# Layer B's attention: a step's filling work ahead of its scores, queries one step later, the output's first pieces two by two

## The chip, the cores and the metric

The kernel runs on one core of one Trainium2 chip. The metric is the device time of one execution in microseconds (us), and for the kernel before it is the median of three runs.

## The reference

A trunk of two layers, 512 tokens, 1024 features, float32. Layer A is latent attention with an MLP behind it, layer B is windowed attention with an MLP behind it; every sublayer is followed by a scaled residual and a layer norm. The change lies in layer B's attention, so that is what is shown (cut):

```python
def _swa(x, w_q, sinks, w_o, k_band, v_band, rel_bias):       # 16 query heads, 4 key/value heads, 64 wide
    q = (x @ w_q).reshape(B, nb, BLOCK, SWA_KV_HEADS, G, SWA_HEAD_DIM)
    s = jnp.einsum('bnqkgd,bnjkd->bnkgqj', q, k_band) * SWA_HEAD_DIM ** -0.5   # block of 128 queries, 256 keys
    s = jnp.where(mask, s + bias, -jnp.inf)
    m = jnp.maximum(s.max(-1), sink)
    p = jnp.exp(s - m[..., None])
    p = p / (p.sum(-1) + jnp.exp(sink - m))[..., None]
    o = jnp.einsum('bnkgqj,bnjkd->bnqkgd', p, v_band).reshape(B, S, 1024)
    return o @ w_o
```

`k_band` and `v_band` hold, for each block of 128 tokens, the keys and values of that block and of the one before it.

## The kernel before

Every product is made of rounded halves: an operand is split into a high half (ScalarE, a copy) and a low half (VectorE or GpSimd, a subtraction), both by the helper `split` (lines 77 and 81), and three matmuls stand for one product, by the helper `group` (line 105). In the profile line 105 is therefore nearly all of TensorE, and lines 77 and 81 are the two halves of a split, told apart by the tile that they write.

TensorE runs its instructions in the order of the program. On the other engines the order is fixed when the kernel is built, by a list of priorities in which earlier code goes first, except where `behind(...)` orders one instruction after another.

Layer B's attention goes head by head in `run_steps`. A unit is a head, `AHEAD_B` is 2, and the steps are u = -2 to 15. In a step stand, for the 16 heads:

- `scores(u + 2)`, here S(u+2): eight matmuls into two PSUM tiles of the tag `mm` (six tiles of that tag for everything). Behind them, off TensorE: four adds of the bias with a maximum (VectorE, line 1332), one small operation `nb` (line 1336), four exponentials (ScalarE, line 1340), a fifth one `ri` (line 1344), a sum and a reciprocal (VectorE, lines 1345 and 1346) and two scalings of `p` (GpSimd, lines 1347 and 1349). The last exponential of line 1340 is kept as `state["exp"]`.
- the filling work, a list of closures with a weight and a due step each. `queries(m, part)`, here Qm.0 and Qm.1: twelve matmuls each, and with the second part the load of a bias tile and the split of the queries of heads 2m and 2m+1 (ScalarE line 1303, VectorE line 1304). `more_values(t)`, here V2 and V3: 24 narrower matmuls each and a split. `proj.part(t, kp)`, here Pt.kp: six matmuls of the output projection, into one PSUM tile for each block t that stays held until the projection ends. P0.2, P1.2 and P2.2 read the attention output of heads 8 to 11.
- `turn(u)`, here T(u): seven transpositions of `p` (lines 1360 and 1362) into two PSUM tiles of the tag `tr`, of which there are two in all, and a split of each into `pth` (ScalarE) and `ptl` (VectorE). The first tile takes four transpositions, the second three.
- `mix(u - 1)`, here M(u-1): eight matmuls with the values, then `low` (ScalarE, line 1391) and `o` (VectorE, line 1392), and after each second head a split into `oh` (ScalarE) and `ol` (GpSimd).

The split of T(u)'s first tile is ordered behind the newest exponentials in the program:

```python
if k2 == 0:
    with behind((state["exp"],)):
        split(pth[:, 0:2, :], ptl[:, 0:2, :], pt)
```

At that point of the program the newest exponentials are those of S(u+2). `fill` is worked off by weight: a closure is called while the weight spent is below the share due by the step, or its own due step has come.

Weights come as a stream: when a chunk is taken, the chunk three further on is loaded (SyncE) into one of two raw tiles and split into one of four pairs of tiles `wh`, `wl`. The chunks of the query weights and the first three of the output projection have their low half made on GpSimd, the later ones on VectorE.

Of the kernel before, what the change touches and what calls it, by code (L numbers as in the profile page):

```python
# [25 lines left out]
SQH, SKVH, SHD = 16, 4, 64  # L26
# [15 lines left out]
AHEAD_S, AHEAD_B = 3, 2  # L42
# [6 lines left out]
def build(tc, nc, io, out):  # L49
    with ExitStack() as top:  # L50
# [11 lines left out]
        def nm(s):  # L62
            n_names[0] += 1
            return f"{s}_{n_names[0]}"

        def bank(cols=512, tag="mm", bufs=6):
            return ps.tile([P, cols], F32, tag=tag, bufs=bufs, name=nm(tag), padded_shape=[P, 512])
# [35 lines left out]
        def group(dst, pairs, first=True, last=True, **kw):  # L103
            for i, (st, mv) in enumerate(pairs):
                pe(nc.tensor.matmul(  # L105
                    dst, st, mv, start=first and i == 0, stop=last and i == len(pairs) - 1, **kw
                ))

        def three(sh, sl, mh, ml):
            return [(sh, mh), (sh, ml), (sl, mh)]  # L110
# [197 lines left out]
        def weights(name):  # L308
            i = state["at"]
            state["at"] += 1  # L310
            while state["next"] < len(stream):
                on_ring = len([j for j in range(i, state["next"] + 1) if not off_ring[j]])
                if on_ring > AHEAD or state["next"] >= state["hold"] or (off_ring[state["next"]] and mlp_pool[0] is None):
                    break
                prep(state["next"])
                state["next"] += 1
            got, wh, wl = ready.pop(i)
            assert got == name
            return wh, wl
# [7 lines left out]
        class Feat:  # L327
# [11 lines left out]
            def turn(self, t):  # L339
                turn_tokens(t, self)  # L340
# [189 lines left out]
                    for t in range(NT):  # L530
                        self.evac(t, slice(512, D), bs[t])

        def run_steps(units, ahead, scores, turn, mix, fill, per, lag, rest):

            total = sum(f[0] for f in fill)
            n, spent, at = len(units), 0.0, 0
            for u in range(-ahead, n):
                if u + ahead < n:  # L540
                    scores(*units[u + ahead])
                target = total * (u + ahead + 1) / (n + ahead)
                while at < len(fill) and (spent < target or fill[at][1] <= u) and fill[at][2] <= u:
                    fill[at][3]()
                    spent += fill[at][0]
                    at += 1
                if u < 0:
                    continue
                turn(*units[u])
                if u >= lag and (u - lag) % per == per - 1:  # L550
                    mix(units[u - lag][0])
            for f in fill[at:]:
                f[3]()
            for f in rest:
                f()
            for u in range(n, n + lag):
                if (u - lag) % per == per - 1:
                    mix(units[u - lag][0])
# [29 lines left out]
        def feat_major(src, w, dst, cols=slice(0, S), ks=range(KD)):  # L588
            wh, wl = w
            for k in ks:  # L590
                kc = slice(k * P, (k + 1) * P)
                group(dst, three(wh[:, kc], wl[:, kc], src.h(k, cols), src.l(k, cols)), k == 0, k == KD - 1)
# [30 lines left out]
        class Factors:  # L623
# [6 lines left out]
            def scratch(self):  # L630
                return self.mp.tile([P, 4, 256], F32, tag="uv", bufs=3, name=nm("uv"))

            def sum(self, n, a11, a12, a21, a22):
                if n == 5:
                    self.a = self.scratch()
                    nc.vector.tensor_sub(self.a, a21, a22)
                    return self.a
                if n == 3:
                    nc.vector.tensor_sub(self.a, self.a, a11)
                    self.b = self.scratch()  # L640
                    nc.vector.tensor_add(self.b, a12, self.a)
                    return self.b
                if n == 7:
                    nc.vector.tensor_sub(self.b, a11, a21)
                    return self.b
                return {1: a11, 2: a12, 4: a22, 6: self.a if n == 6 else None}[n]
# [250 lines left out]
        with tc.tile_pool(name="mla", bufs=1) as mp:  # L897
# [222 lines left out]
            def scores(h, i):  # L1120
                a = heads[h]
                kk = a["k"]
                qh, ql = a["q"]
                n = (i + 1) * P
                tq = slice(i * P, n)
                b = bank()
                p = scratch()
                mask = cmask[:, 512 - n :]
                if i == 0:

                    two = b[:, 0:256].rearrange("p (a b) -> p a b", a=2)
                    group(
                        two, [(qh[:, tq], kk[:, :, :n]), (a["qr"][:, tq], krr[:, :, :n])], True, False,
                        skip_group_check=True,
                    )
                    group(b[:, :n], [(ql[:, tq], kk[:, 0, :n])], False, True, skip_group_check=True)
                    nc.vector.tensor_add(p[:, :n], b[:, n : 2 * n], mask)
                    mask = p[:, :n]
                else:
                    group(  # L1140
                        b[:, :n],
                        three(qh[:, tq], ql[:, tq], kk[:, 0, :n], kk[:, 1, :n])
                        + [(a["qr"][:, tq], khh[:, :n]), (a["qr"][:, tq], kll[:, :n])],
                    )
                if i == 0:
                    for name in ("mx", "nb", "sm", "ri"):
                        a[name] = sp.tile([P, NT], F32, tag=name, bufs=3, name=nm(name))
                mx, nb, sm, ri = a["mx"], a["nb"], a["sm"], a["ri"]
                one = slice(i, i + 1)
                nc.vector.tensor_tensor_reduce(  # L1150
                    out=b[:, :n], in0=b[:, :n], in1=mask, op0=ALU.add, op1=ALU.max,
                    scale=1.0, scalar=NEG, accum_out=mx[:, one],
                )
                nc.vector.tensor_scalar(nb[:, one], mx[:, one], -MLA_SCALE, None, ALU.mult)
                nc.scalar.activation(
                    p[:, :n], b[:, :n], AF.Exp, bias=nb[:, one], scale=MLA_SCALE, accum_out=sm[:, one]
                )
                nc.vector.reciprocal(ri[:, one], sm[:, one])
                nc.vector.tensor_scalar(p[:, :n], p[:, :n], ri[:, one], None, ALU.mult)
                a["p", i] = p  # L1160
# [17 lines left out]
            def mix(h):  # L1178
                vh, vl = v_h[h // 4], v_l[h // 4]
                vc = slice((h % 4) * P, (h % 4 + 1) * P)  # L1180
                pth, ptl = heads[h]["pt"]
                b = bank()
                for kb in range(NT):
                    c = slice(kb * P, S)
                    group(
                        b[:, c], three(vh[:, kb, vc], vl[:, kb, vc], pth[:, kb, c], ptl[:, kb, c]),
                        kb == 0, kb == NT - 1,
                    )
                split(oh[h // 4][:, h % 4, :], ol[h // 4][:, h % 4, :], b)
# [9 lines left out]
            fill = []  # L1199
# [32 lines left out]
        with tc.tile_pool(name="swa", bufs=1) as mp:  # L1232
# [55 lines left out]
            def queries(m, part):  # L1288
                if part == 0:
                    qb[m] = (weights("w_sq"), bank())  # L1290
                w, b = qb[m]
                feat_major(x2, w, b, ks=range(4 * part, 4 * part + 4))
                if part == 1:
                    load_bias(m)
                    with tc.high_priority():
                        query_parts(m, slice(0, S), b)
# [100 lines left out]
            fill = []  # L1397
            for m in range(2, 8):
                for part in range(2):
                    fill.append((2.6, 2 * m - AHEAD_B - 3 + part, -9, lambda m=m, part=part: queries(m, part)))  # L1400
                if m == 2:
                    for t in range(2, NT):
                        fill.append((2.6, 0, -9, lambda t=t: more_values(t)))
            for t, kp, u in ((0, 0, 11), (0, 1, 12), (1, 0, 13), (1, 1, 13), (2, 0, 14), (2, 1, 14), (0, 2, 15), (1, 2, 15), (2, 2, 16)):
                fill.append((1.3 if t < 2 else 0, u, u, lambda t=t, kp=kp: proj.part(t, kp)))
            begin(
                x2, ["w_k"] * 2, [lambda cols, b, m=m: keys(m, cols, b) for m in range(2)],
# [2 lines left out]
            for m in range(2):  # L1410
                for part in range(2):
                    queries(m, part)
            run_steps([(h, 0) for h in range(SQH)], AHEAD_B, scores, turn, mix, fill, 1, 1, [])

        gb = lambda: load_gb("mix", 1)
        with tc.tile_pool(name="mlp1", bufs=1) as mp:
# [114 lines left out]
```

## Time and profile before

| | |
|---|---|
| runs | 997.11, 997.43, 998.21 us; median 997.43 us |
| the profiled execution | 997.58 us, of which 995.8 us are the span of its instructions |
| granted TensorE clock | 0.999 |
| TensorE busy | 983.9 us (99% of the span) |
| VectorE, ScalarE, GpSimd busy | 772.3, 555.2, 215.4 us |

Times of rows are microseconds from the start of the span. A row of a timeline has start, duration, engine, line, operation, the tile written and the tiles read, shapes, a count, and in brackets the idle time before it with what ended it. A row of the chain has start, duration, engine, tile and line. A row of stretches has the stretch, its length, the busy time of TensorE, of its weight loads, of VectorE, ScalarE and GpSimd with instruction counts, the granted clock, the share of the DMA engines and GB/s. A row of waits has who waited for whom, the total, the number of times and the longest. A row of groups has line, engine, operation, tiles, shapes and count, then the total busy time and the mean in ns.

### The profile page before, as it was taken

Reading aid. Unit: us, or ns where it says so; the run is one execution under the profiler, and the core shown is the slowest. Engines: PE = TensorE matmul, PEld = TensorE weight load, DVE = VectorE, ACT = ScalarE, POOL = GpSimd, SP = SyncE. Lnnn points to the kernel's source line nnn. Section 1 sums busy time; section 2 is a strip of 40 time slices with the busy share of each in tenths; the row PEclk is TensorE's granted clock in tenths of the full one; section 3 lists DMA queues with packets and bytes.
Section 4 is the critical chain, followed back from the end, with each engine's and each line's share of the span. In section 5 each row is a group of like instructions: output and inputs, shape, how many; then the busy total and the mean of one; then the engine's idle time right before and its main releaser. Section 6 shows DMA issues by size and latency. Waiting matters only on the chain.

```text
span 995.8 us, 15827 instructions
## 1 busy us (share of the span) xinstructions
PE 983.9 (99%) x6103; PEld 887.2 (89%) x6103; DVE 772.3 (78%) x1242; ACT 555.2 (56%) x850; POOL 215.4 (22%) x203
## 2 busy tenths in 40 slices
PE   9999999999999999999999999999999999999997
PEld 9888887998999999998898998889998999999986
DVE  6589858999768769786686778698985886898756
ACT  5556644467547547646145798546763663664620
POOL 1231001121212212210002775112131122023000
PEclk9999999999999999999999999999999999999999
DMA  7421228389789978964132212359698698798422
GB/s 261 144 88 44 70 99 241 93 180 235 141 181 241 170 170 218 225 108 148 64 106 96 85 65 75 105 149 211 179 204 186 165 217 173 166 264 143 119 90 85
DMA packets 60679, 149.55 MB, mean 150 GB/s; under 512 B 5260, under 2 KB 10301, under 8 KB 60605
## 3 DMA queue, kind: packets, MB, share of 16 engines
q0 software_dynamic: 24320, 58.73, 33.0%
q1 hardware_dynamic: 36140, 89.56, 26.7%
q8 instruction: 48, 0.79, 0.3%
q10 hardware_dynamic: 144, 0.26, 0.1%
q14 instruction: 27, 0.21, 0.1%
HBM read 146.41 MB, written 4.22 MB: 151 GB/s over the span
## 4 chain that ended last, share of the span: by engine, by line
PE 93%; DVE 2%; DMA 2%; issue 1%; ACT 1%; POOL 0%; DVEq 0%; SPq 0%; POOLq 0%; ACTq 0%
PE mm L105 85%; PE tr L105 5%; PE tr L1171 1%; DMA wq<-in_up 1%; PE tr L678 1%; PE tr L1360 1%; DMA raw<-in_w_v 1%; ACT wh L77 1%; DVE wl L81 0%; PE tr L1362 0%; DVE x L440 0%; DMA xraw<-in_xT 0%; DVE mm L1332 0%; DVE x L437 0%; POOL wq L200 0%
## 5 line engine op out<-in xcount | busy, mean ns | idle before, releaser
L105 PE MATMUL mm<-wh,fac 128*128 128x512 f32 (+1 forms) x944 | 292.6, 386 | 0.0
L77 ACT ACTIVATE wh<-wq 128x1024 fp32r<-128x1024 f32 x164 | 173.7, 1060 | 183.7 <-PE mm L105 128.3
L81 DVE TENSOR_TENSOR wl<-wq,wh 128x1024 fp32r<-128x1024 f32 x164 | 199.6, 1221 | 70.3 <-ACT wh L77 69.4
L105 PE MATMUL mm<-xth,wh 128*128 128x256 f32 (+1 forms) x928 | 243.4, 290 | 0.0
L105 PE MATMUL mm<-xth,wl 128*128 128x256 f32 (+1 forms) x800 | 233.2, 292 | 0.0
L105 PEld LDWEIGHTS mm<-wh,fac 128*128 128x128 f32 x944 | 176.2, 188 | 35.4 <-DVE fac L81 0.6
L105 PE MATMUL mm<-xtl,wh 128*128 128x256 f32 (+1 forms) x672 | 197.1, 293 | 0.0
L105 PE MATMUL mm<-wl,fac 128*128 128x512 f32 (+1 forms) x472 | 182.3, 386 | 0.0
L105 PEld LDWEIGHTS mm<-xth,wh 128*128 128x128 f32 x928 | 168.6, 192 | 3.1
L105 PEld LDWEIGHTS mm<-xth,wl 128*128 128x128 f32 x800 | 153.2, 192 | 2.6
L77 ACT ACTIVATE wh<-raw 128x1024 fp32r<-128x1024 f32 (+3 forms) x86 | 85.1, 990 | 97.6 <-PE mm L105 57.3
L200 POOL DMA_DIRECT2D wq<-in_up x64 | 77.5, 1228 | 259.4 <-DVE wl L81 191.9
L105 PEld LDWEIGHTS mm<-xtl,wh 128*128 128x128 f32 x672 | 128.7, 192 | 3.0
L81 DVE TENSOR_TENSOR wl<-raw,wh 128x1024 fp32r<-128x1024 f32 (+2 forms) x66 | 77.1, 1174 | 36.1 <-ACT wh L77 35.8
L105 PEld LDWEIGHTS mm<-wl,fac 128*128 128x128 f32 x472 | 88.8, 188 | 16.7
L200 POOL DMA_DIRECT2D wq<-in_down x48 | 42.0, 875 | 187.3 <-DVE wl L81 181.4
L81 POOL TENSOR_TENSOR wl<-raw,wh 128x1024 fp32r<-128x1024 f32 (+2 forms) x20 | 41.2, 2062 | 88.1 <-ACT wh L77 82.1
L105 PE MATMUL mm<-wh,oh 128*128 128x512 f32 x128 | 50.9, 397 | 0.0
L105 PE MATMUL mm<-wh,ol 128*128 128x512 f32 x128 | 50.1, 391 | 0.0
L105 PE MATMUL mm<-wl,oh 128*128 128x512 f32 x128 | 50.0, 391 | 0.0
L413 POOL TENSOR_TENSOR rs<-mv,half 128x1 f32<-128x1 f32 x16 | 9.9, 620 | 168.0 <-DVE mv L434 167.9
L578 DVE TENSOR_TENSOR x<-mm,x 128x512 f32<-128x512 f32 (+1 forms) x49 | 32.9, 675 | 15.8 <-PE mm L105 15.7
(222 smaller groups left out, 1816.0 us busy)
## 6 DMA issues: line engine op xcount, KB each, us to landing
wq<-in_up POOLq DMA_DIRECT2D x64, 512.0 KB, 8.6
wq<-in_down POOLq DMA_DIRECT2D x48, 512.0 KB, 6.9
wq<-in_up SPq DMA_DIRECT2D x32, 512.0 KB, 6.6
raw<-in_down SPq DMA_DIRECT2D x28, 512.0 KB, 6.6
wq<-in_down SPq DMA_DIRECT2D x24, 512.0 KB, 5.0
raw<-in_up SPq DMA_DIRECT2D x16, 512.0 KB, 4.2
raw<-in_w_o SPq DMA_DIRECT2D x8, 512.0 KB, 5.1
raw<-in_w_sq SPq DMA_DIRECT2D x8, 512.0 KB, 3.2
```

The source lines that it names most:

```text
L77: high = nc.scalar.activation(dst_h, src, AF.Copy)
L81: low = (engine or nc.vector).tensor_sub(dst_l, src, f32(dst_h))
L105: pe(nc.tensor.matmul(dst, st, mv, start=first and i == 0, stop=last and i == len(pairs) - 1, **kw))
L200: nc.gpsimd.dma_start(half(a, jp), chunk(*more, jp), accum_op=ALU.add)
L413: nc.gpsimd.tensor_tensor(r, v, half, ALU.pow)
L578: nc.vector.tensor_add(xs[t][:, c], b, xs[t][:, c])
L678: pe(nc.tensor.transpose(pt[:, a, :], xs[t][:, k * P : (k + 1) * P], ident))
L1171: pe(nc.tensor.transpose(pt[:, kb * P : (kb + 1) * P], p[:, kb * P : (kb + 1) * P], ident))
L1360: pe(nc.tensor.transpose(pt[:, a, 0:P], p[:, kb, P:256], ident))
```

## The change

With `fill_first` a step calls its filling work before its scores. The queries' due steps are one later. The list of output pieces has other steps and another order. The layer A attention, which also uses `run_steps`, is as it was.

```diff
-        def run_steps(units, ahead, scores, turn, mix, fill, per, lag, rest):
+        def run_steps(units, ahead, scores, turn, mix, fill, per, lag, rest, fill_first=False):
...
             for u in range(-ahead, n):
-                if u + ahead < n:
+                if u + ahead < n and not fill_first:
                     scores(*units[u + ahead])
                 target = total * (u + ahead + 1) / (n + ahead)
                 while at < len(fill) and (spent < target or fill[at][1] <= u) and fill[at][2] <= u:
                     fill[at][3]()
                     spent += fill[at][0]
                     at += 1
+                if u + ahead < n and fill_first:
+                    scores(*units[u + ahead])
...
-                    fill.append((2.6, 2 * m - AHEAD_B - 3 + part, -9, lambda m=m, part=part: queries(m, part)))
+                    fill.append((2.6, 2 * m - AHEAD_B - 2 + part, -9, lambda m=m, part=part: queries(m, part)))
...
-            for t, kp, u in ((0, 0, 11), (0, 1, 12), (1, 0, 13), (1, 1, 13), (2, 0, 14), (2, 1, 14), (0, 2, 15), (1, 2, 15), (2, 2, 16)):
+            for t, kp, u in ((0, 0, 12), (0, 1, 12), (1, 0, 13), (1, 1, 13), (0, 2, 14), (1, 2, 14), (2, 0, 15), (2, 1, 15), (2, 2, 16)):
...
-            run_steps([(h, 0) for h in range(SQH)], AHEAD_B, scores, turn, mix, fill, 1, 1, [])
+            run_steps([(h, 0) for h in range(SQH)], AHEAD_B, scores, turn, mix, fill, 1, 1, [], True)
```

Worked through by hand, the weights and due steps give these orders on TensorE:

| step | before | after |
|---|---|---|
| -2, -1 | S0 Q2.0, S1 Q2.1 | Q2.0 S0, Q2.1 S1 |
| 0 | S2 V2 V3 T0 | V2 V3 S2 T0 |
| 1 | S3 Q3.0 T1 M0 | S3 T1 M0 |
| 2 | S4 Q3.1 T2 M1 | Q3.0 S4 T2 M1 |
| 3 | S5 Q4.0 T3 M2 | Q3.1 S5 T3 M2 |
| ... | ... | ... |
| 10 | S12 Q7.1 T10 M9 | Q7.0 S12 T10 M9 |
| 11 | S13 P0.0 T11 M10 | Q7.1 S13 T11 M10 |
| 12 | S14 P0.1 T12 M11 | P0.0 P0.1 S14 T12 M11 |
| 13 | S15 P1.0 P1.1 T13 M12 | P1.0 P1.1 S15 T13 M12 |
| 14 | P2.0 P2.1 T14 M13 | P0.2 P1.2 T14 M13 |
| 15 | P0.2 P1.2 T15 M14 | P2.0 P2.1 T15 M14 |
| end | P2.2 M15 | P2.2 M15 |

## The prediction, as put on record before the change was run

> **What bounds the kernel now.** I read the page first, then the waits of TensorE over the whole run, then the stretches of layer B's attention, then its chain and its timelines.
>
> ```profile
> span 995.8 us, 15827 instructions
> PE 983.9 (99%) x6103; PEld 887.2 (89%) x6103; DVE 772.3 (78%) x1242; ACT 555.2 (56%) x850; POOL 215.4 (22%) x203
> ```
> ```profile
> PE tr L1360 <- DVE ptl L81: 1.7, 3, 0.9
> ```
> ```profile
> 551.93:604.91 52.98, 52.98 (x345) 47.54 (x343) 41.20 (x146) 44.37 (x130) 36.82 (x30) 1.00 0.28 96
> 604.91:616.21 11.30, 9.58 (x68) 8.25 (x67) 10.21 (x34) 10.30 (x32) 4.87 (x6) 1.00 0.15 49
> ```
> TensorE never stops between 551.93 and 604.91, the steps 0 to 9. It stops in the next 11.30 us, steps 10 to 12, and those are the three waits of the second fence: transpositions that wait for VectorE to give a `tr` tile back. So the change can gain at most these waits, and lose wherever it makes new ones. Their true size, from the starts on TensorE:
>
> ```profile
> 607.55 0.40 PE L105 MATMUL mm<-wh,oh 128*128 128x512 f32 x1
> ...
> 608.71 0.39 PE L105 MATMUL mm<-wh,ol 128*128 128x512 f32 x1
> 609.98 0.30 PE L1360 MATMUL tr<-ident,p 128*128 128x128 f32 x1 [0.89 <-DVE ptl L81]
> ...
> 610.34 0.27 PE L1362 MATMUL tr<-ident,p 128*128 128x128 f32 x1
> 610.79 0.30 PE L1360 MATMUL tr<-ident,p 128*128 128x128 f32 x1 [0.18 <-DVE ptl L81]
> ...
> 614.73 0.27 PE L1362 MATMUL tr<-ident,p 128*128 128x128 f32 x1
> 615.66 0.33 PE L1360 MATMUL tr<-ident,p 128*128 128x128 f32 x1 [0.65 <-DVE ptl L81]
> ```
> Six matmuls of P0.0 start 0.23 apart (607.55 to 608.71 are five gaps), so T11 was due at 608.94 and came at 609.98: 1.04. Transpositions follow each other after 0.11: T11's second tile was due at 610.45, 0.34 late; T12's second tile at 614.84, 0.82 late. With the slightly longer first transposition after each wait (0.03, 0.03, 0.05) that is **2.3 us**, all there is to gain: 0.23% of the run. A measurement of this kernel can tell about 0.2%, 2.0 us, from no change.
>
> **The change, part by part.** No matmul and no transfer is added or removed. What moves is the distance on TensorE between a step's scores and its transpositions. One whole step before:
>
> ```profile
> 553.63 0.40 PE L105 MATMUL mm<-xth,wh 128*128 128x512 f32 x1
> ...
> 556.38 0.27 PE L1360 MATMUL tr<-ident,p 128*128 128x128 f32 x1
> ...
> 557.06 0.36 PE L105 MATMUL mm<-pth,vv 128*128 128x256 f32 x1
> ...
> 558.03 0.27 PE L105 MATMUL mm<-skh,q 128*128 128x128 f32 x1
> ...
> 559.01 0.40 PE L105 MATMUL mm<-xth,wh 128*128 128x512 f32 x1
> ```
> Half a query product (or a pair of output pieces) takes 2.75, T 0.68, M 0.97, S 0.98: a step is 5.38. The code orders the split of T(u)'s first tile behind the exponentials of S(u+2), and T(u+1) needs that tile back. The timeline shows the order at work:
>
> ```profile
> 611.41 0.49 ACT L77 ACTIVATE pth<-tr 128x384 fp32r<-128x384 f32 x1 [0.88 <-PE tr L1360]
> ...
> 612.32 0.36 ACT L1340 ACTIVATE p<-mm,nb 128x128 f32<-128x128 f32 x1
> ...
> 614.01 0.31 ACT L1344 ACTIVATE ri<-nb,sink 128x4 f32<-128x4 f32 x1
> 614.20 0.61 ACT L77 ACTIVATE pth<-tr 128x512 fp32r<-128x512 f32 x1
> ```
> T11's second tile (384 wide) is copied at once, its first (512 wide), filled earlier, only after the four exponentials and `ri` of S13. So a chain hangs on every S(u+2): scores end, `ri` starts, copy, subtraction, tile free, T(u+1). Call the time that TensorE gives this chain the leash. Before, in a full step, it is filling, T, M, S, filling: 2.75 + 0.68 + 0.97 + 0.98 + 2.75 = 8.13. After, T, M, filling, S: **5.38**. If the second tile is freed first, as above, the late one is needed only by the second half of T(u+1), 0.44 later: 5.82.
>
> How long is the chain? From its last piece: S13's `ri` at 614.01 to T12's second tile at 615.66 is 1.65. The first piece, scores' end (the start of what follows them on TensorE) to `ri`, differs:
>
> ```profile
> 542.49 0.40 PE L105 MATMUL mm<-xth,wh 128*128 128x512 f32 x1
> 538.81 0.40 PE L105 MATMUL mm<-xth,wh 128*128 128x512 f32 x1
> 602.16 0.40 PE L105 MATMUL mm<-xth,wh 128*128 128x512 f32 x1
> ```
> ```profile
> 546.06 0.30 ACT L1344 ACTIVATE ri<-nb,sink 128x4 f32<-128x4 f32 x1
> 542.98 0.30 ACT L1344 ACTIVATE ri<-nb,sink 128x4 f32<-128x4 f32 x1
> 608.14 0.30 ACT L1344 ACTIVATE ri<-nb,sink 128x4 f32<-128x4 f32 x1
> ```
> S1, with the engines nearly idle: 3.57, chain 5.2. S0, which stands right behind a finished pair of queries (the place that every second scores has in the new order): 4.17, chain 5.8. S12, in the full flow: 5.98, chain 7.6 or more. Before, 7.6 fits the leash of 8.13. After, only the idle cases fit.
>
> *Step 0 to 1.* In the new order nothing fills step 1, and M comes after T1: S2 T0 S3 T1. The leash of S2 is T and S, 1.66, and 2.10 for the second tile. The chain is S1's at best, 5.2. T1 loses **3.1**. Before, V2 and V3 lay between S2 and T0, from 546.17 to 551.93, and S2's exponentials were done by then:
>
> ```profile
> 546.17 0.28 PE L105 MATMUL mm<-wh,xth 128*128 128x256 f32 x1
> ...
> 551.93 0.27 PE L1360 MATMUL tr<-ident,p 128*128 128x128 f32 x1
> ```
> ```profile
> 553.34 0.68 DVE L81 TENSOR_TENSOR ptl<-tr,pth 128x512 fp32r<-128x512 f32 x1
> ```
> T0's place on TensorE is unchanged, so nothing gives this back.
>
> *Steps 3, 5, 7, 9, 11*, where queries finish right ahead of the scores, their split in front of the bias adds on VectorE: the chain is 5.8 at best, 0.0 over the leash; with S12's 7.6 it is 1.8 over. Such a wait delays only the step after, whose own chain then has more room, so I count five waits, not eleven. I take 0.5 each, nearer to S0, because the arrangement is S0's; the 0.5 is an estimate of what stands in VectorE's queue there and not in S0's, the add `o` of an earlier head:
>
> ```profile
> L1392 DVE TENSOR_TENSOR o<-mm,low 64x512 f32<-64x512 f32 x15 | 10.2, 682 | 0.4
> ```
> Five times 0.5 is **2.5**, between 0 and 9.
>
> *The end.* Steps 11 to 13 get 2.75 of filling each instead of 1.38, 1.38 and 2.75. T11 and T12 no longer come early, and the 2.3 go. What is late next there is S13's chain: VectorE's split of an output weight still falls in,
>
> ```profile
> 605.97 1.23 DVE wl L81
> ```
> one step later, since its tile is freed by Q7.1. The leash of S13 is 5.38 in both orders; before, its chain took 8.1 (607.55 to 615.66). So up to 1.2 of the 2.3 can come back; with 0.3 on the other side of my estimate for that step I leave it in the range.
>
> *Edits at no cost.* p: a head's transpositions come two steps after its scores, 10.8 instead of 13.5; the slowest p,
>
> ```profile
> 615.55 1.47 POOL L1349 TENSOR_TENSOR p<-p,ri 128x768 f32<-128x768 f32 x1
> ```
> was ready 9.5 after S13's end (607.55): 1.3 to spare, and if that cover went each us over would be lost at one T. P0.2 and P1.2, one step earlier, read the low half of heads 10 and 11:
>
> ```profile
> 616.21 4.62 PE mm L105 x28
> ```
> ```profile
> 620.95 1.28 POOL L81 TENSOR_TENSOR ol<-o,oh 128x512 fp32r<-128x512 f32 x1 [1.07 <-ACT oh L77]
> ```
> it was done at 622.23, 6.0 after T12; in the new order P0.2 starts 6.3 after T12 (0.97 + 2.75 + 0.98 + 0.68 + 0.97) and needs it about 1 us later still. The bias loads on SyncE's queue move with the queries:
>
> ```profile
> DMA to landing us min/median/max: 2.7/2.8/5.2
> ```
> They wait for their slot, not for the queries, and have a step (5.38) from Qm.1 to the scores that read them, so at worst 0; the weight loads ahead of them keep their order. Six `mm` tiles: at a scores' start two of the last scores, a query tile or two and one of M may be live; they come free with the same exponentials, so they wait when the chain waits, not in addition.
>
> *Sum*, against the profiled execution's 997.58: -2.3 + 3.1 + 2.5 = +3.3, 1000.9. That execution lies 0.15 above the median of the runs, 997.43, so I predict **1000.8**.
>
> [...] The rows first:
>
> ```profile
> 549.27 2.41 POOL L81 TENSOR_TENSOR wl<-raw,wh 128x1024 fp32r<-128x1024 f32 x1
> ...
> 553.85 4.75 POOL L81 TENSOR_TENSOR wl<-raw,wh 128x1024 fp32r<-128x1024 f32 x2
> ```
> ```profile
> 550.08 1.63 DVE L1345 TENSOR_TENSOR sm<-sm,ri 128x4 f32<-128x4 f32 x1 [1.36 <-ACT ri L1344]
> ```
> A sum over 128x4 takes 1.63 and ends at 551.71, 0.03 after GpSimd's split of a weight ends. It then cost nothing. In the new order the sum of S2 is due at about 551.93 + 3.6 + 0.4 = 555.9, inside the pair of splits that ends at 558.60, and T0's subtraction stands behind it on VectorE: it could be held for 2.5, and T1 with it. [...]
>
> **The rivals.**
> - *No waits at the queries* (0.17): the five chains stay at S0's 5.8 within 5.82. For it: S0. Against: S12. -2.3 + 3.1 = +0.8, 998.2, no change.
> - *Not slower* (0.12): the order behind the exponentials doesn't bind at step 0, T0's copy goes first and T1 waits only for a subtraction. It decides at 2.1 after T0's end: the tile given back by then, no large wait. For it: before, T0's first tile was subtracted at 554.02, 2.1 after T0's start, where T1 would need it after 1.66. Against: S2's exponentials were past by then, and the rows at 611.41 to 614.20. With those 0.5 for the wait and none at the queries, 995.6.
> - *The flow as it is now* (0.09): all five chains keep S12's 7.6. For it: S12 is the row of the busy flow. Against: its slack of 8.13 let it drift. -2.3 + 3.1 + 9.0 = +9.8, 1007.2.
> [...]
>
> **How the numbers follow.** The forecast has 0.50, with 0.25 to 1.2 per chain: 999.5 to 1004.2. The range goes from 997.0 to 1006.0: it leaves out the rival below and most of the busy flow. Slower by over 0.2% (over 999.4): forecast 0.50, interface 0.12, flow 0.09: 0.71. Faster by over 0.2% (under 995.4): 0.05, the better part of the second rival. The rest, 0.24, is within.
>
> **What would show it.** A wait of about 3 us at T1, for VectorE's `ptl`, in one or two pieces; waits of 0.2 to 1.2 at T4, T6, T8, T10 and T12 for the same releaser; none at T11. `ri` should start 3.5 to 5 after the scores' end. I am wrong on the mechanism if T1 waits under 1 us, or if its releaser is GpSimd's p; wrong on the size if the later waits come at every step or at none.

## The result: 1.6% slower

The kernel after takes 1013.8 us (median of 4 runs, 1011.98 to 1014.44), before 997.4 us (4 runs): ratio 1.016, 95% interval 1.0148 to 1.0173. 1000.8 was predicted, with a range up to 1006.0; the time lies outside it.

The page of the kernel after, its head and the row of the granted clock over 40 slices:

```profile
span 1012.4 us, 15797 instructions
PE 990.2 (98%) x6103; PEld 892.1 (88%) x6103; DVE 774.6 (77%) x1242; ACT 555.1 (55%) x850; POOL 216.5 (21%) x203
PEclk9999999999999999999999998999999999999999
```
The same 6103 matmuls are busy 6.3 us longer (990.2 against 983.9), and one slice has a clock under 0.9. The view of waits has one line for layer B's attention, where before it had 1.7 us in 3 waits:

```profile
PE tr L1362 <- DVE ptl L81: 12.2, 8, 3.2
```
The timeline of TensorE shows them one by one (line 1362 is the old line 1360):

```profile
555.02 0.30 PE L1362 MATMUL tr<-ident,p 128*128 128x128 f32 x1 [0.83 <-DVE ptl L81]
558.66 0.33 PE L1362 MATMUL tr<-ident,p 128*128 128x128 f32 x1 [3.01 <-DVE ptl L81]
578.32 0.33 PE L1362 MATMUL tr<-ident,p 128*128 128x128 f32 x1 [1.68 <-DVE ptl L81]
589.90 0.33 PE L1362 MATMUL tr<-ident,p 128*128 128x128 f32 x1 [0.57 <-DVE ptl L81]
602.64 0.33 PE L1362 MATMUL tr<-ident,p 128*128 128x128 f32 x1 [1.73 <-DVE ptl L81]
614.21 0.33 PE L1362 MATMUL tr<-ident,p 128*128 128x128 f32 x1 [0.56 <-DVE ptl L81]
628.39 0.48 PE L1362 MATMUL tr<-ident,p 128*128 128x128 f32 x1 [3.17 <-DVE ptl L81]
641.96 0.33 PE L1362 MATMUL tr<-ident,p 128*128 128x128 f32 x1 [0.69 <-DVE ptl L81]
```
In order: T1 twice, T4, T6, T8, T10, T12, T14. A transposition normally starts 0.11 after the one before it, although it lasts 0.27, so each wait costs 0.16 more than its bracket: 4.2, 1.8, 0.7, 1.9, 0.7, 3.3 and 0.9, together 13.5. The wait at T11 is gone. Behind the two long waits stands something else, in the stretches of the same kernel (the column after GpSimd's is the granted clock):

```profile
559.00:560.00 1.00, 1.00 (x8) 1.00 (x7) 0.16 (x1) 1.00 (x6) 0.81 (x1) 0.68 0.89 352
560.00:561.00 1.00, 1.00 (x6) 0.90 (x5) 0.88 (x3) 0.97 (x3) 0.57 (x2) 0.50 0.00 0
561.00:562.00 1.00, 1.00 (x4) 0.81 (x3) 1.00 (x2) 0.27 (x1) 1.00 (x1) 0.50 0.00 0
562.00:563.00 1.00, 1.00 (x4) 0.76 (x4) 0.05 (x1) 0.00 (x0) 0.26 (x1) 0.62 0.00 0
563.00:564.00 1.00, 1.00 (x6) 0.82 (x5) 0.00 (x0) 0.00 (x0) 0.00 (x0) 1.00 0.00 0
...
628.00:630.00 2.00, 1.61 (x8) 1.61 (x9) 0.68 (x3) 2.00 (x9) 1.53 (x2) 0.50 0.04 8
630.00:632.00 2.00, 2.00 (x8) 1.79 (x8) 1.53 (x3) 0.98 (x3) 1.82 (x2) 0.50 0.00 0
632.00:634.00 2.00, 2.00 (x6) 1.53 (x5) 0.30 (x1) 0.63 (x1) 0.95 (x1) 0.50 0.00 0
634.00:635.00 1.00, 1.00 (x4) 0.80 (x4) 0.00 (x0) 0.00 (x0) 0.32 (x1) 0.78 0.00 0
```
After each, the granted clock of TensorE is 0.50, and towards the end of each stretch VectorE, ScalarE and GpSimd stand mostly idle. What the rows lack to 1.00 adds up to 1.7 us of work at 559 to 563 and 3.2 at 628 to 635, some 0.2 of it still waiting: about 4.7. So -2.3 + 13.5 + 4.7 = 15.9 of the 16.6 us by which the span grew (995.8 to 1012.4); 0.7 is not placed.

### The profile page after: what moved, and what is told of

Its sections match the earlier page's. It is cut to its first block, busy times and chain, and to the rows that moved or that the text cites. A ratio compares the mean times of both kernels' runs of the same rounds, so it can differ in the third digit from the quotient of the medians.

```text
span 1012.4 us, 15797 instructions
## 1 busy us (share of the span) xinstructions
PE 990.2 (98%) x6103; PEld 892.1 (88%) x6103; DVE 774.6 (77%) x1242; ACT 555.1 (55%) x850; POOL 216.5 (21%) x203
## 4 chain that ended last, share of the span: by engine, by line
PE 92%; DVE 3%; ACT 2%; DMA 1%; issue 1%; POOL 0%; SPq 0%; DVEq 0%; POOLq 0%; ACTq 0%
PE mm L105 84%; PE tr L105 5%; PE tr L1173 1%; PE tr L680 1%; PE tr L1362 1%; ACT p L1342 1%; DMA wq<-in_up 1%; DVE ptl L81 1%; DMA raw<-in_w_v 1%; DVE mm L1334 1%; DVE wl L81 0%; ACT wh L77 0%; PE tr L1364 0%; DVE x L440 0%; DVE x L437 0%
```

## The experiments

Theory L is the prediction's: the split of T(u)'s first tile follows the exponentials of S(u+2) (this order is called the tie below), and in the new order TensorE comes for that tile 5.38 us after the scores' end instead of 8.13. All ratios are to the kernel before, run on the same chip, with 95% intervals; the kernel after stands at 1.016.

**The order within a step undone, the new due steps kept.**

```diff
-run_steps(..., AHEAD_B, scores, turn, mix, fill, 1, 1, [], True)
+run_steps(..., AHEAD_B, scores, turn, mix, fill, 1, 1, [])
```


> The new kernel with the old order in a step (scores, filling, T, M) and the new due steps. Theory L (the leash: scores' end to the transposition that needs the first tile back is 5.38 instead of 8.13): the leash is 8.13 again, so the eight waits of 12.2 us and both stretches of half clock go; T11 and T12 are no longer early, so before's 2.3 go too; step 1 has no filling, T1 follows T0 by S3 alone and waits about 0.5. 997.4 - 2.3 + 0.5 = 995.6. Rival D (the due steps and the output pieces' order make the waits, as queries come closer to their scores): 1008 or more.

Measured 1002.34 us, ratio 1.0046 (1.0031 to 1.0061). The waits for `ptl` shrank to one of 0.4, and the clock is 0.998 in the mean, as L says. But the time is 6 to 7 us over what it gave, for reasons that L has nothing of; the view of waits, and the first such row of TensorE's timeline:

```profile
PE mm L105 <- DVE q L1306: 3.3, 5, 1.1
...
PE mm L105 <- DVE o L1394: 0.7, 1, 0.7
...
PE tr L1362 <- DVE ptl L81: 0.4, 1, 0.4
```
```profile
568.08 0.33 PE L105 MATMUL mm<-skh,q 128*128 128x128 f32 x1 [0.60 <-DVE q L1306]
```
S6 now follows Q3.1 by T3 and M2 alone, 1.65 us, and waits for the split of its own queries; so do S8, S10, S12 and S14. By the starts on TensorE these five cost 4.4, and the wait for `o`, ahead of P1.0, about 1.0. The due steps are bad by themselves in the old order, and only there: with filling first, half a query product lies between.

**The new order with the old due steps and the old list of output pieces** (both lists as in the diff's removed lines).

> The new order in a step with the old due steps and the old list of output pieces. Theory L: the filling of step 1 is back ahead of S3, so the leash of S2 is T, Q3.0, S = 4.41 (4.85 for a second tile) instead of 1.66; T1 waits about 1 instead of 4.3 and the clock stays at 1.00 there (1.6 more); the waits at every second T stay, and steps 11 and 12 with one output piece have a leash of 4.0, so T12 and T13 wait 2 to 4. 1013.8 - 3.3 - 1.6 + 0 to 2 = 1009 to 1011. Rival D: near 997.

Measured 1014.32 us, ratio 1.0165 (1.015 to 1.018). T1's wait fell to 1.5 and the clock stayed up there, as expected, but the total, given as 1009 to 1011, did not fall. The view of waits:

```profile
PE tr L1362 <- DVE ptl L81: 12.8, 7, 3.6
```
The waits sit at T1, T3, T5, T7, T9, T11 and T14 now, up to 3.6, with the same releaser, and the clock falls behind T3 and T11. My sum held the other waits fixed, and they are not. What the two runs say together: the order within a step makes the `ptl` waits, whichever lists it is given.

**The split freed from the exponentials, in the kernel after.**

```diff
-with behind((state["exp"],)):
-    split(pth[:, 0:2, :], ptl[:, 0:2, :], pt)
+split(pth[:, 0:2, :], ptl[:, 0:2, :], pt)
```


> The new kernel without the order of the first tile's split behind the exponentials; nothing else. Theory L: the chain from the scores to the next transpositions is cut, the waits at T1, T4, T6, T8, T10, T12 and T14 go but for a rest of some tenths where VectorE is busy, no clock loss: 996 to 999. Rival Q (queues: VectorE and ScalarE are simply too late in the new order, whatever the order of the split): most of the 12.2 us of waits stay, 1008 or more.

Measured 997.61 us over 10 runs, ratio 1.0001 (0.9991 to 1.001): the whole loss is gone. The view of waits has for layer B's attention, with 0.2 at T1 for `nb`, only

```profile
PE tr L1362 <- DVE ptl L81: 1.0, 1, 1.0
PE mm L105 <- DVE o L1393: 0.7, 1, 0.7
```
at T1 and at S14. So it is the tie and not VectorE's or ScalarE's load as such: the engines do the same work here. This is the run that decides for L.

**The same edit in the kernel before.**

> The kernel before without the order of the first tile's split behind the exponentials. Theory L: before, the same chain made the waits at T11 and T12 (leash 6.75 and 5.38), so they go, 2.3: 995.1 to 996. Rival: those waits came from VectorE's weight split and backlog alone, and stay; or the free order puts splits ahead of exponentials and makes p late: 997.4 to 999.

Measured 999.80 us over 9 runs, ratio 1.0023 (1.0013 to 1.0033): slower, as the second rival had it, though beyond its 999 and with no T that waits for p. T12 no longer waits and T11's wait fell from 1.4 to 0.8, but matmuls of the filling wait for exponentials,

```profile
PE mm L105 <- ACT p L1340: 1.6, 6, 0.7
```
which read the `mm` tiles: the scores' tiles come free later, as I read it because the copies of `tr` tiles are now taken first. In the old order the tie is worth some 2 us, in the new one it costs 16.

**What makes the chain so long.** The chain of S5, whose end is the start of T3 at 570.65, in the kernel after; VectorE, then ScalarE, then VectorE again:

```profile
572.26 0.68 DVE L1306 TENSOR_TENSOR q<-mm,q 64x512 fp32r<-64x512 f32 x1
572.87 0.41 DVE L1334 CUSTOM_DVE_ANT_0 mm<-mm,bias 128x256 f32<-128x256 f32 x1
573.32 0.56 DVE L81 TENSOR_TENSOR ptl<-tr,pth 128x384 fp32r<-128x384 f32 x1
573.79 0.67 DVE L1394 TENSOR_TENSOR o<-mm,low 64x512 f32<-64x512 f32 x1
574.39 0.20 DVE L1338 TENSOR_SCALAR nb<-mm,sink 128x4 f32<-128x4 f32 x1
```
```profile
576.40 0.30 ACT L1346 ACTIVATE ri<-nb,sink 128x4 f32<-128x4 f32 x1
```
```profile
577.60 0.66 DVE L81 TENSOR_TENSOR ptl<-tr,pth 128x512 fp32r<-128x512 f32 x1
```
The last bias add is done at 573.3; `nb`, which needs nothing else, starts at 574.39, behind a subtraction and `o`. `ri` starts 5.75 after the scores' end, T4's second tile comes at 578.32, 7.67 after it. The leash is 5.82: 1.85 too late, the wait at T4 to within 0.01.

I first gave the bias adds and `nb` priority:

```diff
+with tc.high_priority():
     ...  # the four bias adds with their maxima
     nc.vector.tensor_scalar(nb, mx, sink8[:, h : h + 1], -SWA_SCALE, ALU.max, ALU.mult)
```


> The new kernel with the four bias adds and nb of the scores given high priority, so that VectorE takes them ahead of an older head's o, ptl and of the queries' split. Theory Q2 (the chain is 7.6 instead of 5.8 because those stand between the bias adds and nb on VectorE): the chain shortens by 1.2 or more, the waits at T4 and T8 go from 2.0 to under 0.8, those of 0.8 at T6 and T10 to about 0: 1013.8 - 3 to 5 = 1009 to 1011. Rival: ScalarE (copies of weights and queries ahead of the exponentials) sets the chain, waits as they were, 1013 to 1014.5.

Measured 1013.54 us, ratio 1.0155 (1.0138 to 1.0172). It tests nothing: VectorE's order around S5 stayed what it was, `nb` behind `o`. The two rows, and the unchanged waits:

```profile
572.99 0.67 DVE L1395 TENSOR_TENSOR o<-mm,low 64x512 f32<-64x512 f32 x1
573.58 0.20 DVE L1339 TENSOR_SCALAR nb<-mm,sink 128x4 f32<-128x4 f32 x1
```
```profile
PE tr L1363 <- DVE ptl L81: 12.2, 8, 3.2
```
So the next run orders them outright.

```diff
-nc.vector.tensor_scalar(nb, ...)
+state["nb"] = nc.vector.tensor_scalar(nb, ...)
...
+with behind((state["nb"],)):
     ...  # VectorE's subtraction for the second tr tile; in mix, VectorE's add to o
```


> The new kernel with VectorE's o and its subtraction for the second transposed tile ordered behind nb of the newest scores. High priority alone had left the order of VectorE as it was. Theory Q2 (these two, 0.67 + 0.56, stand between the bias adds and nb and make the chain 7.6): the waits at T4 and T8 fall from 1.85 to 0.6 to 1.2 (a queries' split of 0.69 can slip in front instead), those at T6 and T10 from 0.73 to 0.2, T12 by 1.2, to 2.1, and there the clock stays up: 1013.8 - 3 to 4.5 - 2.6 = 1007 to 1008.5. Rival (ScalarE sets the chain): no change.

Measured 1009.03 us, ratio 1.0118 (1.0105 to 1.0132), 4 us less than the kernel after by the ratios. T4, T6, T8, T10 and T12 on TensorE's timeline:

```profile
575.12 0.33 PE L1362 MATMUL tr<-ident,p 128*128 128x128 f32 x1 [0.62 <-DVE ptl L81]
587.34 0.33 PE L1362 MATMUL tr<-ident,p 128*128 128x128 f32 x1 [1.21 <-DVE ptl L81]
598.98 0.33 PE L1362 MATMUL tr<-ident,p 128*128 128x128 f32 x1 [0.62 <-DVE ptl L81]
611.20 0.33 PE L1362 MATMUL tr<-ident,p 128*128 128x128 f32 x1 [1.21 <-DVE ptl L81]
624.17 0.33 PE L1362 MATMUL tr<-ident,p 128*128 128x128 f32 x1 [1.96 <-DVE ptl L81]
```
T4 and T8 lost 1.1 each and T12 1.2, as expected, but the clock still fell behind T12, where I expected it to stay up (1.7 us). That and T6 and T10 put the time above the 1007 to 1008.5 that I gave. T6 and T10 gained 0.65 where I expected a loss; I had said that a queries' split of 0.69 could slip in front of `nb`, for T4 and T8. VectorE's rows have it so for T6: the split at 582.50 stands right ahead of `nb` at 583.23, while in the kernel after it stands behind `nb` (586.12 and 585.87), and `nb` comes 0.55 later behind its scores, which is most of the 0.65.

**VectorE's weight split at T12**, moved to GpSimd in the kernel after, and in the kernel before.

```diff
-POOL_O, POOL_SO = (0, 2), (0, 1, 2)
+POOL_O, POOL_SO = (0, 2), (0, 1, 2, 3)
```


> The new kernel with the low half of the fourth output weight made on GpSimd instead of VectorE. Theory L: VectorE's 1.39 us between the bias adds of S13 goes, the wait at T12 falls from 3.3 to 1.9, and at that length the clock does not fall there (2.6 or more): 1013.8 - 4 to 5 = 1009 to 1010. Rival: the split is not in the chain, or GpSimd (2.4 us) makes p14 late: 1013 to 1015.

Measured 1009.73 us, ratio 1.0129 (1.0115 to 1.0143). T12's row and the stretch behind it:

```profile
626.14 0.33 PE L1362 MATMUL tr<-ident,p 128*128 128x128 f32 x1 [1.73 <-DVE ptl L81]
```
```profile
628.00:630.00 2.00, 2.00 (x10) 1.62 (x9) 1.50 (x4) 1.79 (x6) 1.03 (x2) 1.00 0.00 0
```
The wait fell from 3.3 to 1.9 and the clock stayed at 1.00 there, as expected, in the profiled execution; the mean clocks of the four executions, 0.994 to 0.997, suggest that it was not so in each. This is the term that the prediction left in the range as "up to 1.2".

> The kernel before with that same split on GpSimd. Theory: VectorE's 1.23 is in the chain of S13 there too; the waits at T11 and T12 (2.3) fall by about 1.2: 996.3 to 996.6. Rival: GpSimd's 2.4 us stand ahead of p13 or p14, which come late by 1 or more: 997.5 to 999.

Measured 997.11 us over 11 runs, ratio 0.9998 (0.9989 to 1.0007). Before's three waits became one of 1.0 at T11 and one of 0.9 of the filling for exponentials: no gain that can be told, though the split was in that chain too.

**Step 1 filled.**

```diff
-fill.append((2.6, 0, -9, lambda t=t: more_values(t)))
+fill.append((2.6, t - 2, -9, lambda t=t: more_values(t)))
```


> The new kernel with V3 in step 1 instead of step 0: V2 S2 T0, then V3 S3 T1 M0. Nothing else moves on TensorE. Theory L: the leash of S2 is T, V3, S = 4.5 instead of 1.66, the chain stays some 5.3 to 6, so T1 waits 0.4 to 1.5 instead of 4.3, the clock stays at 1.00 there (1.6), all later waits stay: 1013.8 - 2.8 to 3.9 - 1.6 = 1008.3 to 1009.4. Rival: the wait at T1 is not a matter of TensorE's distance and stays, 1013 to 1014.

Measured 1011.45 us, ratio 1.014 (1.0126 to 1.0154). T1's wait is 0.6, and the clock stayed up there, yet 1008.3 to 1009.4 was expected. T0, 2.9 us earlier on TensorE, now waits for p,

```profile
PE tr L1364 <- POOL p L1351: 1.1, 1, 1.1
...
PE tr L1362 <- POOL p L1349: 0.2, 1, 0.2
```
and T2 waits 1.2. The clock, too, fell at another place, behind T8, at the same wait as in the kernel after, where it had stayed up:

```profile
599.75 0.33 PE L1362 MATMUL tr<-ident,p 128*128 128x128 f32 x1 [1.73 <-DVE ptl L81]
```
```profile
600.00:602.00 2.00, 2.00 (x12) 2.00 (x11) 0.04 (x1) 2.00 (x10) 1.08 (x1) 0.50 0.05 8
```
It lost 1.7 us there, and behind T12 1.7 instead of 3.4. So what T1 gave was taken back for the most part, and of the 2.7 us that are left of its span some 1.7 are the shorter drop at T12. With the tie removed as well:

> The new kernel without that order and with V3 in step 1. Without the order alone the run took 997.6, with waits of 1.4 at T1 and 0.9 at S14. Theory L: the wait at T1 goes, the rest stays: 996.2 to 996.6, a gain of about 0.1% on before. Rival: V3 next to T1 makes M0 wait for the split of its values, 997 to 998.

Measured 998.03 us over 11 runs, ratio 1.0008 (0.9999 to 1.0017): no gain, for the same wait at T0, not for the one at M0 that I had named. No version here beats the kernel before.

**The clock.** Useless matmuls in the time in which TensorE waits, in the kernel after: eight ahead of T1 and of T12, then fourteen ahead of T1 alone.

```diff
 def turn(h, _):
     p = ps_of[h]
+    if h in (1, 12):          # second run: h == 1
+        d = bank().rearrange("p (a b) -> p a b", a=4)
+        group(d, [(zeros, zeros[:, None, :].broadcast_to([P, 4, P]))] * 8)      # second run: 14
```


> The new kernel with eight useless matmuls on zeros (8 x 0.23 = 1.8 us of TensorE) right ahead of T1 and of T12, in the time in which TensorE waits there; they add work that the reference doesn't have. Theory C (a wait of over 3 us lets the granted clock fall to 0.5 for some 3 to 6 us after it): T1 and T12 come no later, the clock stays at 1.00, and the 1.6 us at 560 to 563 and 2.6 us or more at 629 to 635 are saved: 1009 to 1010. Rival N (the low clock is an accident of the profile or costs nothing): 1013.8, or 1015 to 1017 if the matmuls on zeros delay what follows.

Measured 1010.79 us, ratio 1.0123 (1.0106 to 1.014). T1 and T12 came no later. 1009 to 1010 was expected, with both drops gone. The stretches behind T1 and behind T12:

```profile
560.00:561.00 1.00, 1.00 (x5) 0.91 (x5) 0.87 (x3) 0.95 (x3) 0.56 (x2) 0.50 0.00 0
...
628.00:630.00 2.00, 1.59 (x13) 1.55 (x14) 0.69 (x3) 2.00 (x9) 1.55 (x2) 1.00 0.00 0
```
At T12 the clock held and its loss went; at T1, where 2.3 us of idle time were left, it fell all the same.

> The new kernel with fourteen useless matmuls on zeros (14 x 0.23 = 3.2 us, added work) ahead of T1 alone, so that TensorE stands idle there for under 1.2 us; with eight the clock still fell to 0.50 from 559 to 562 after 2.3 us of waiting. Theory C (idle time ahead of it lets the clock fall): the clock stays at 1.00 after T1, T1's second tile comes no later, 1.6 us saved: 1012.2. Rival Z (matmuls on zeros do not count as work): the clock falls all the same, 1013.8 or a little more.

Measured 1010.61 us, ratio 1.0137 (1.0123 to 1.0151). Behind T1:

```profile
560.00:561.00 1.00, 1.00 (x6) 0.83 (x5) 1.00 (x2) 0.27 (x1) 1.00 (x1) 1.00 0.00 0
```
The clock held behind T1, and M0 and the filling after it took 1.6 us less than in the kernel after. The ratio fell by more (1.0137 against 1.016, with intervals that just touch), and in the profiled execution the drop behind T12 cost 1.7 instead of 3.4, too, at the same wait of 3.3 and without any edit there; so not all of the difference is the work of these matmuls. The mean clocks of all four executions bear both runs out: 0.997 to 0.998 with eight, 0.996 to 0.997 with fourteen, 0.992 to 0.994 in the kernel after. So in these runs the half clock was a cost of idle time, paid after the wait, and matmuls on zeros in its place kept the clock up: 1.00 behind T12 with eight of them (628 to 630) and 1.00 behind T1 with fourteen (560 to 561), where the kernel after has 0.50 in both stretches.

## Why the prediction was wrong

- *All there is to gain is 2.3*: right in size, and T11's wait went. T12's did not: it grew from 0.8 to 3.3. The prediction saw that S13's leash is 5.38 in both orders and that VectorE's weight split falls into it, and still booked the full 2.3.
- *T1, 3.1*: right in place and kind, measured 4.2. I took the first piece of the chain from S1, 3.57; S2's `ri` came 4.75 after its scores, because S3's bias adds, the split of V3 and T0's second tile stood on VectorE between its own adds and `nb`.
- *Five waits at every second transposition, at T4 to T12*: right in place, releaser and count (with a sixth, 0.9, at T14). The leash of 5.82 was right to within 0.01. **The step that failed is the size of these five: 0.5 each was booked, 2.5 in all, and 8.5 was measured.** I had two rows for the chain, S0's 5.8 with idle engines and S12's 7.6 in the busy flow, and chose the near-idle one because the arrangement matched. T4's chain took 7.67, S12's value: what lengthens it is the queue on VectorE. With `nb` ahead of the subtraction and `o`, 1.1 of T4's 1.8 went. My rival "the flow as it is now", given 0.09, had 9.0 for these five; its sum is near, but not its parts, which are 1.8, 0.7, 1.9, 0.7 and 3.3 instead of 1.8 each.
- *The clock* was missing, a term put at nothing without a reason: 4.7. The five waits (6.0 more than booked), the clock (4.7), T1 (1.1) and T14 (0.9) make 12.7 of the 13.0 us by which the forecast missed. With the clock, T14 and T1, that rival's 1007.2 becomes 1013.9, where the median is 1013.8; that it meets to 0.1 is luck, since its five waits are 0.5 too large, 0.7 is not placed, and the clock's part differs between executions.
- *"Interface", 0.12 among the chances*, stands for 2.5 more at step 1, the sum of S2 held until GpSimd's pair of splits ends, and T1 with it. No run shows these 2.5: the sum came only 0.19 before the splits' end, behind `ri`, took 0.20 and ended 0.01 after them. S0's sum took 0.83 and ended 0.02 after a split of GpSimd, where the median of the 16 sums is 0.16; why, no run here tests.

```profile
546.64 2.40 POOL L81 TENSOR_TENSOR wl<-raw,wh 128x1024 fp32r<-128x1024 f32 x1 [4.78 <-ACT wh L77]
...
552.93 4.68 POOL L81 TENSOR_TENSOR wl<-raw,wh 128x1024 fp32r<-128x1024 f32 x2
...
548.23 0.83 DVE L1347 TENSOR_TENSOR sm<-sm,ri 128x4 f32<-128x4 f32 x1
...
557.42 0.20 DVE L1347 TENSOR_TENSOR sm<-sm,ri 128x4 f32<-128x4 f32 x1 [0.89 <-ACT ri L1346]
```
- *"Not slower"* fell with the first wait: the tie binds at step 0.
- *Edits at no cost* held in the kernel after: no T waits for p, no output piece for `ol`. The cover of p is thin, though: it was gone at T0 when V3 was moved.

## What to carry to other kernels

When an order is changed, look for ties between instructions that were put there for the old order, and measure the distance that the bound engine leaves each tie, before and after; here 8.13 became 5.38 against a chain of 7.7. Take that chain's length from the busy flow of the trace, not from its idle beginning, since the queues come along. And a wait of two or three microseconds on TensorE can cost more than its length: here each one that brought the clock down to 0.50 cost 1.7 or 3.4 on top, while one of 2.4 left it at 1.00.

## What the runs showed of the hardware

Some idle waits of TensorE were followed by a granted clock of 0.50. In the kernel after, the clock lost 1.7 us after T1, which is 3.4 us at half, and 3.4 us after T12, from 627 on, which is 6.8 us at half. Length alone doesn't decide: waits of 1.8 and 1.9 (T4, T8) left it at 1.00 in the kernel after, and the same wait at T8 brought it down in the run with step 1 filled; with `nb` first one of 2.1 at T12 brought it down, with the old lists one of 2.4 at T7 did not. The stretch behind T12 with `nb` first, then T7's row and the stretch behind it with the old lists:

```profile
626.00:628.00 2.00, 2.00 (x6) 1.53 (x5) 1.48 (x4) 1.81 (x6) 1.00 (x2) 0.50 0.00 0
```
```profile
598.71 0.33 PE L1362 MATMUL tr<-ident,p 128*128 128x128 f32 x1 [2.28 <-DVE ptl L81]
```
```profile
600.00:602.00 2.00, 2.00 (x11) 1.65 (x11) 1.85 (x5) 1.34 (x3) 1.48 (x2) 1.00 0.47 186
```
What decides between waits of one length, no run here shows. The waits that brought the clock down were of 1.9 (T8, step 1 filled), 2.1 (T12, `nb` first), 2.7 (T3, the old lists) and 3.3 us (T12, the kernel after), among others.
